# Three instead of two of eight column-block pairs of a gated feed-forward layer in seven block products

## The chip, the cores and the metric

One core of a Trainium2 chip. The metric is the device time of one execution in microseconds (us). The engines are PE (TensorE: matmuls, with PEld for its weight loads), DVE (VectorE), ACT (ScalarE), POOL (GpSimd) and SP (SyncE, whose queue issues the loads of the weights).

## The reference

Two layers over 256 tokens of width 2048, float32. Each layer is feed-forward 1, a mixer (stick-breaking attention in the first layer, causal pooling in the second), feed-forward 2, each behind a scaled residual and followed by a layer norm. There are thus four feed-forward layers, and these are what the change is about:

```python
def swiglu(x, w_in, w_out):
    a, gate = jnp.split(x @ w_in, 2, axis=-1)      # w_in: 2048 x 8192, split into 4096 + 4096
    return (jax.nn.silu(a) * gate) @ w_out         # w_out: 4096 x 2048
...
    x = layer_norm(DEEPNORM_ALPHA * x + FFN_RESIDUAL * swiglu(x, *ffn1[i]), *ln1[i])
    x = layer_norm(DEEPNORM_ALPHA * x + mixers[i](x), *ln2[i])
    x = layer_norm(DEEPNORM_ALPHA * x + FFN_RESIDUAL * swiglu(x, *ffn2[i]), *ln3[i])
```

## The kernel before, in words

Activations stay on the chip, transposed: features on the 128 partitions, the 256 tokens along the free dimension. To keep float32 accuracy each operand is split in two: ACT casts it to a rounded high part, DVE subtracts that from the operand to give the low part (`parts`, L323, for the weights here; L140 and L141 in `chunk`). High times high, high times low and low times high are accumulated in PSUM.

`ffn_in` (L447) computes the 8192 columns of `w_in` as eight groups of 512 features (one block of 512 columns of the first half and its partner in the gate's half):

- Group 0 comes first, by two calls of `gemm`, whose hooks also finish the layer norm before it.
- The middle groups go by **column units**. `feature(t)` (L520) is a block of 128 features: two units, one for the first half's 128 columns and one for the gate's. A unit is `column` (L327): one load of 1 MB, two casts and two subtractions of 128x1024, 32 matmuls (16 of 128x512, high weight with both parts of the activations, and 16 of 128x256, low weight with the high part) into one PSUM bank, an ACT copy of the bank (L350), one DVE add (L524), and a silu or, every second time, a multiply (L535). A group of 512 features is eight units.
- The last `SEVENS` groups go by **seven block products** (`Seven`): the 256 tokens are two halves of 128, the 2048 inputs two halves of 1024 and the two partner blocks of columns the third pair, so that a group is a 2x2 by 2x2 block product, done with seven products instead of eight and sums before and behind. `prepare` (L360) makes the sums of activations once per layer. `run` (L376) goes through eight steps, each with one load of 1 MB (L383), the split of the plain blocks, three combinations of weight blocks (L400), their splits, and seven products of three 128x512 matmuls each (L422 to L424), accumulated over the steps in seven PSUM banks. Behind the last step an ACT copy and seven DVE adds (L434) combine the banks. The result has tokens on the partitions; `gated` (L470) multiplies it with the gate and puts off eight PE transposes (L481) and two ACT copies, the "late" part.

Between the products of a run the code interleaves column units: `run` calls `between(i, h)` (L559) after the first four (h = 0) and the last three products (h = 1) of step i, except at the very end. The units before, between and behind the runs are taken in order from one list (`unit`, L543). Before the first run some units come early; the late part of a run comes in the first step of the next one. At the end `settle` (L458) splits the gated products for the output matmul, partly into the places of the activations' sums.

The buffers that count: three raw blocks of weights (`raws`), six pairs for split weights (`whis`, `wlos`), two for combinations (`sums`), four `wide` tiles, and eight PSUM banks, of which a run holds seven.

What sets the order: the code is not issued as it is written. A planner takes the instructions by priority (their order in the code), simulates times with its own costs, gives out buffers, and so writes each engine's order. Each engine then works through its list in that order.

Of the kernel before, what the change touches and what calls it, by code (L numbers as in the profile page):

```python
# [21 lines left out]
INNER = HEADS * P  # L22
WINDOWS = (2, 4, 8, 16)

SEVENS = 2
PARTS = ('', '_columns', '_seven')
ALPHA = 4 ** 0.25
SB_SCALE = P ** -0.5
# [10 lines left out]
def trunk(ctx: ExitStack, tc: tile.TileContext, a: dict, out: bass.AP):  # L39
# [407 lines left out]
    def ffn_in(w_in, w_columns, w_seven, norm, hooks=None):  # L447
# [69 lines left out]
        seven.prepare(1)  # L517
        todo = list(range(4, 4 * (ng - SEVENS)))

# [18 lines left out]
        units = []  # L538
# [4 lines left out]
        def unit():  # L543
            if not units:
                return
            go = units.pop(0)
            if held:
                go(held.pop())
            else:
                held.append(go())  # L550

        early = len(units) - 16 * SEVENS
        for _ in range(early // 2):
            unit()
        if hooks:
            hooks()
        lates = []

        def between(i, h):  # L559
            unit()  # L560
            if lates and (i, h) == (0, 1):
                lates.pop()()

        for grp in range(ng - SEVENS, ng):
            acts, gates = seven.run(w_seven, grp - ng + SEVENS, between)
            unit()
            lates.append(gated(grp, silu(acts, acts), gates))
# [9 lines left out]
    def ffn(p, i, ln, norm):  # L577
        gs = ffn_in(*(a[f'{p}ffn{i}_w_in' + x] for x in PARTS), norm)
        if norm is None:
            nc.sync.dma_start(vecs, a['vecs'])  # L580
        return sublayer_end(a[f'{p}ffn{i}_w_out'], gs, 0.5, f'{p}{ln}_g', f'{p}{ln}_b')
# [162 lines left out]
    def last(p, norm):  # L744
# [5 lines left out]
        def turn():  # L750
            for q in range(4):
# [6 lines left out]
                for m in range(2):  # L758
                    nc.scalar.copy(z[q][:, m, :], ps[m])

        gs = ffn_in(*(a[f'{p}ffn2_w_in' + x] for x in PARTS), norm, hooks=turn)
        for i, name in enumerate((f'{p}ln3_g', f'{p}ln3_b')):
            gb = res.tile([P, 4, 2 * W], F32, tag=f"xs{i}", name=f"gb{i}")
# [105 lines left out]
```

## Time and profile before

| | us |
|---|---|
| median of 3 runs | 2654.95 (2654.46 to 2655.19) |
| the profiled execution | 2653.92 |
| its span, first to last instruction | 2652.2 |
| PE busy in the span | 2632.2 |
| DVE busy | 1964.3 |
| ACT busy | 1476.5 |

The profile records one execution. Busy times of an engine are the union of its instructions' times; a matmul's recorded end is modelled and overlaps the start of the next. A row of a group of instructions reads: line, engine, operation, output and inputs, shape, count, busy time in us and mean ns of one, then the engine's idle time before them and what ended it. A row of a window reads: the stretch in us from the span's start, its length, then busy us (and instructions) of each engine, the granted clock, the share of the DMA engines and GB/s.

### The profile page before, as it was taken

The page shows a single profiled execution, that of the slowest core. Times are in us where ns is not written, and L with a number is a line of the kernel's source. Part 1 is how long each engine was busy: PE and PEld are TensorE (multiplying, and loading weights), DVE is VectorE, ACT ScalarE, POOL GpSimd, SP SyncE. Part 2 cuts the span into 40 slices and gives each one's busy share as a digit, 9 for nine tenths or more (in the row PEclk, how much of TensorE's full clock was granted, in tenths as well). Part 3 has the DMA queues.
Part 4 walks back from the last instruction along what each step waited for, and adds up shares of the span by engine and source line. Part 5 has one row for each costly group of instructions (what it writes and reads, how often), then busy time and mean ns, then how long its engine had stood idle before and what let it go on. Part 6 is the DMA issues. An engine that isn't in the chain of part 4 may idle for free.

```text
span 2652.2 us, 37769 instructions
## 1 busy us (share of the span) xinstructions
PE 2632.2 (99%) x15148; PEld 2303.4 (87%) x15148; DVE 1964.3 (74%) x2650; ACT 1476.5 (56%) x2094; POOL 11.9 (0%) x28
## 2 busy tenths in 40 slices
PE   9999999999999999999999999999999999999998
PEld 8888888899998888888988888889888998888886
DVE  8778766585689787665797886657878797888545
ACT  6556554466576565544655565445555575566432
POOL 0000000000000000000000000000000000000000
PEclk9999999999999999999999999999999999999999
DMA  7555555554455555555455555554555545555653
GB/s 269 193 178 206 182 201 187 189 178 165 151 177 191 189 195 192 201 183 197 169 189 198 192 190 191 191 191 165 201 188 177 191 159 191 192 192 207 221 195 121
DMA packets 71518, 499.54 MB, mean 188 GB/s; under 512 B 7984, under 2 KB 8624, under 8 KB 12080
## 3 DMA queue, kind: packets, MB, share of 16 engines
q1 hardware_dynamic: 70704, 495.05, 53.6%
q8 instruction: 118, 1.93, 0.3%
q0 software_dynamic: 640, 2.10, 0.2%
q14 instruction: 56, 0.46, 0.1%
HBM read 495.02 MB, written 2.10 MB: 187 GB/s over the span
## 4 chain that ended last, share of the span: by engine, by line
PE 98%; ACT 1%; DVE 0%; DMA 0%; SPq 0%; issue 0%; DVEq 0%; ACTq 0%
PE pc L341 23%; PE ps L164 21%; PE pc L345 12%; PE ps L167 10%; PE ps L159 4%; PE ps L158 4%; PE ps L160 4%; PE p L422 4%; PE p L423 4%; PE p L424 4%; PE y L805 2%; PE y L806 2%; PE y L804 2%; PE v L660 1%; PE v L658 1%; PE v L659 1%
## 5 line engine op out<-in xcount | busy, mean ns | idle before, releaser
L341 PE MATMUL pc<-xs,whi 128*128 128x512 f32 x2560 | 914.5, 397 | 3.7 <-ACT col L350 2.9
L141 DVE TENSOR_TENSOR wlo<-raw,whi 128x1024 fp32r<-128x1024 f32 (+1 forms) x498 | 596.7, 1202 | 423.8 <-ACT whi L140 423.0
L140 ACT CAST whi<-raw 128x1024 fp32r<-128x1024 f32 (+1 forms) x498 | 510.5, 1033 | 550.1 <-PE ps L164 343.8
L345 PE MATMUL pc<-xs,wlo 128*128 128x256 f32 x2560 | 694.0, 281 | 0.0
L341 PEld LDWEIGHTS pc<-xs,whi 128*128 128x128 f32 x2560 | 481.6, 189 | 116.8 <-ACT col L350 10.4
L325 DVE TENSOR_TENSOR wlo<-raw,whi 128x1024 fp32r<-128x1024 f32 (+1 forms) x448 | 503.0, 1144 | 47.4 <-ACT whi L324 28.9
L164 PE MATMUL ps<-g,whi 128*128 128x512 f32 x1536 | 534.9, 394 | 0.0
L324 ACT CAST whi<-raw 128x1024 fp32r<-128x1024 f32 (+1 forms) x448 | 432.8, 989 | 173.1 <-PE pc L341 153.4
L345 PEld LDWEIGHTS pc<-xs,wlo 128*128 128x128 f32 x2560 | 483.7, 189 | 13.0
L167 PE MATMUL ps<-g,wlo 128*128 128x256 f32 x1536 | 427.8, 280 | 0.0
L164 PEld LDWEIGHTS ps<-g,whi 128*128 128x128 f32 x1536 | 287.2, 187 | 65.3
L167 PEld LDWEIGHTS ps<-g,wlo 128*128 128x128 f32 x1536 | 289.7, 189 | 1.1
L350 ACT COPY col<-pc 128x512 f32<-128x512 f32 x160 | 93.9, 588 | 224.0 <-PE pc L341 222.0
L159 PE MATMUL ps<-xs,whi 128*128 128x258 f32 (+1 forms) x768 | 218.3, 284 | 0.0
L158 PE MATMUL ps<-xs,whi 128*128 128x258 f32 (+1 forms) x768 | 217.6, 283 | 0.0
L160 PE MATMUL ps<-xs,wlo 128*128 128x258 f32 (+1 forms) x768 | 216.5, 282 | 0.0
L164 PE MATMUL ps<-xs,whi 128*128 128x512 f32 x512 | 178.9, 396 | 0.9 <-ACT whi L140 0.9
L160 PEld LDWEIGHTS ps<-xs,wlo 128*128 128x128 f32 x768 | 146.2, 190 | 0.0
L159 PEld LDWEIGHTS ps<-xs,whi 128*128 128x128 f32 x768 | 145.4, 189 | 0.2
L158 PEld LDWEIGHTS ps<-xs,whi 128*128 128x128 f32 x768 | 144.6, 188 | 0.0
L167 PE MATMUL ps<-xs,wlo 128*128 128x256 f32 x512 | 141.0, 281 | 1.6 <-DVE wlo L141 1.6
L524 DVE TENSOR_TENSOR col<-col 128x256 f32<-128x256 f32 x160 | 67.7, 423 | 77.6 <-ACT col L350 76.6
(196 smaller groups left out, 3581.5 us busy)
## 6 DMA issues: line engine op xcount, KB each, us to landing
raw<-in_l_ffn_w_in_columns SPq DMA_DIRECT2D x160, 1024.0 KB, 4.9
raw<-in_l_ffn_w_out SPq DMA_DIRECT2D x127, 1024.0 KB, 4.9
raw<-in_l_ffn_w_in_seven SPq DMA_DIRECT2D x64, 1024.0 KB, 5.2
raw<-in_l_pool_w_in SPq DMA_DIRECT2D x32, 1024.0 KB, 4.9
raw<-in_l_ffn_w_in SPq DMA_DIRECT2D x28, 1024.0 KB, 4.9
raw<-in_l_sb_w_qkv SPq DMA_DIRECT2D x24, 1024.0 KB, 4.9
raw<-in_l_pool_w_out SPq DMA_DIRECT2D x16, 1024.0 KB, 4.9
raw<-in_l_sb_w_o SPq DMA_DIRECT2D x8, 1024.0 KB, 5.0
```

Source lines behind the costliest of these rows:

```text
L140: nc.scalar.copy(hi[:, i], src)
L141: nc.vector.tensor_tensor(out=lo[:, i], in0=src, in1=hi[:, i].bitcast(F32), op=ALU.subtract)
L158: nc.tensor.matmul(ps[:, :one], hi[:, cs], x[:, 0, :one], start=first, stop=False)
L159: nc.tensor.matmul(ps[:, :one], hi[:, cs], x[:, 1, :one], start=False, stop=False)
L160: nc.tensor.matmul(ps[:, :one], lo[:, cs], x[:, 0, :one], start=False, stop=last)
L164: nc.tensor.matmul(ps.rearrange("p (h n) -> p h n", h=2), hi[:, cs], x, start=first, stop=last)
L167: nc.tensor.matmul(ps[:, :T], lo[:, cs], x[:, 0], start=False, stop=False)
L324: nc.scalar.copy(hi, src)
L325: nc.vector.tensor_tensor(out=lo, in0=src, in1=hi.bitcast(F32), op=ALU.subtract)
L341: nc.tensor.matmul(ps.rearrange("p (h n) -> p h n", h=2), his[k], whole[k], start=k == 0, stop=k == KT - 1)
L345: nc.tensor.matmul(ps[:, :T], los[k], whole[k][:, 0], start=False, stop=False)
L422: nc.tensor.matmul(p, xh, hi, start=i == 0, stop=False)
```

## The change

The number of groups done in seven products goes from two to three (`SEVENS`, which also sets how the weights are laid out in memory before the launch). The units left per layer go from 40 to 32. Where the code took half of the units that the runs leave as early ones, it now takes four (the same number as before). Between the products of a run a unit now comes after the second part of each step (h = 1) and, in the last step, after the first part; before, one came after either part.

```diff
-SEVENS = 2
+SEVENS = 3
...
-        early = len(units) - 16 * SEVENS
-        for _ in range(early // 2):
+        for _ in range(4):
             unit()
...
         def between(i, h):
-            unit()
+            if h == 1 or i == 7:
+                unit()
             if lates and (i, h) == (0, 1):
                 lates.pop()()
```

In the code's order a layer was: four units, a run with 15 units between, one unit, a second such run, and five units behind it (one at once, one after the first `settle`, three at the end). Now it is: four units, three runs with eight units between and one unit after each, and one more after the first `settle`.

## Rows read from the trace of the kernel before

**Rows 1.** Page, head and part 1: busy us, share, instructions of each engine.

```profile
span 2652.2 us, 37769 instructions
...
PE 2632.2 (99%) x15148; PEld 2303.4 (87%) x15148; DVE 1964.3 (74%) x2650; ACT 1476.5 (56%) x2094; POOL 11.9 (0%) x28
```

**Rows 2.** Page, part 4: the chain that ended last, by engine.

```profile
PE 98%; ACT 1%; DVE 0%; DMA 0%; SPq 0%; issue 0%; DVEq 0%; ACTq 0%
```

**Rows 3.** Page, part 6: DMA issues, with count, KB each, us to landing.

```profile
raw<-in_l_ffn_w_in_columns SPq DMA_DIRECT2D x160, 1024.0 KB, 4.9
...
raw<-in_l_ffn_w_in_seven SPq DMA_DIRECT2D x64, 1024.0 KB, 5.2
```

**Rows 4.** Windows of the first and second feed-forward layer: both runs, the rest.

```profile
75.45:204.83 129.38, 129.38 (x682) 110.16 (x680) 100.93 (x118) 71.73 (x89) 0.00 (x0) 1.00 0.54 192
204.83:330.74 125.91, 125.49 (x658) 106.05 (x657) 102.36 (x131) 76.04 (x107) 0.00 (x0) 1.00 0.54 191
811.11:942.34 131.23, 129.95 (x682) 110.10 (x680) 107.99 (x130) 75.95 (x98) 0.00 (x0) 1.00 0.55 192
942.34:1068.26 125.92, 125.48 (x658) 106.06 (x657) 102.47 (x131) 75.83 (x107) 0.00 (x0) 1.00 0.54 191
330.74:359.82 29.08, 29.08 (x170) 25.49 (x169) 23.31 (x33) 19.35 (x32) 0.00 (x0) 1.00 0.64 220
```

**Rows 5.** Chain in order of time: start, us, the transposes behind the second run.

```profile
347.30 0.66 PE gt L481 x6
```

**Rows 6.** Groups of instructions by shape: DVE's work in units and runs.

```profile
L325 DVE TENSOR_TENSOR wlo<-raw,whi 128x1024 fp32r<-128x1024 f32 x384 | 461.9, 1220 | 45.6 <-ACT whi L324 28.7 <-PE pc L345 14.4 <-issue 0.5
...
L400 DVE TENSOR_TENSOR ta<-raw 128x1024 f32<-128x1024 f32 x64 | 78.2, 1222 | 18.8 <-DMA raw<-in_l_ffn_w_in_seven 18.1
...
L524 DVE TENSOR_TENSOR col<-col 128x256 f32<-128x256 f32 x160 | 67.7, 423 | 77.6 <-ACT col L350 76.6
...
L400 DVE TENSOR_TENSOR tb<-raw,ta 128x512 f32<-128x512 f32 x64 | 43.8, 685 | 0.1
...
L434 DVE TENSOR_TENSOR c<-p,su 128x512 f32<-128x512 f32 x16 | 11.0, 685 | 0.0
```

**Rows 7.** Timeline of DVE, end of first layer: start, us, instruction, count.

```profile
325.05 1.42 DVE L108 TENSOR_TENSOR g<-gw,g 128x256 fp32r<-128x256 f32 x4
...
329.68 1.28 DVE L434 TENSOR_TENSOR c<-p,u 128x512 f32<-128x512 f32 x2
...
338.56 3.49 DVE L325 TENSOR_TENSOR wlo<-raw,whi 128x1024 fp32r<-128x1024 f32 x3
```

**Rows 8.** Timelines of ACT and PE, second layer's first step; in brackets idle before.

```profile
813.23 1.05 ACT L324 CAST whi<-raw 128x1024 fp32r<-128x1024 f32 x1 [0.81 <-PE p L423]
...
814.71 0.58 ACT L350 COPY col<-pc 128x512 f32<-128x512 f32 x1
...
815.34 0.50 PE L341 MATMUL pc<-xs,whi 128*128 128x512 f32 x1 [1.26 <-ACT col L350]
```

**Rows 9.** Windows around the start of the second layer's runs.

```profile
773.16:829.18 56.02, 54.74 (x340) 48.75 (x339) 56.02 (x85) 41.95 (x70) 0.00 (x0) 1.00 0.55 188
788.61:811.11 22.50, 22.50 (x130) 19.66 (x129) 22.50 (x38) 11.73 (x17) 0.00 (x0) 1.00 0.50 167
811.11:827.05 15.94, 14.66 (x70) 11.78 (x69) 15.94 (x22) 13.26 (x19) 0.00 (x0) 1.00 0.50 174
```

**Rows 10.** Waits over the whole span: who, on whom, us, times, longest.

```profile
ACT whi L324 <- PE pc L341: 204.6, 129, 4.1
DVE wlo L325 <- ACT whi L324: 93.9, 102, 2.1
```

## The prediction

> **What bounds the kernel now.** I read the page first: TensorE is busy 99% of the span, VectorE 74%, ScalarE 56% [rows 1], and the chain that ended last lies 98% on TensorE [rows 2]. So the reader is to see a kernel that is a row of matmuls with hardly a hole; only fewer or shorter matmuls, or new holes, can change it. Next come the weights: each block of 1 MB lands about 5 us after its issue [rows 3]. The change reads the same megabytes in another form (a group is eight blocks either way: 160 and 64 of the two kinds now, 128 and 96 then), all issued by the same queue, so the total of DMA stays.
>
> Then I cut the first and second feed-forward layers into stretches [rows 4]: from the first seven-product matmul to that of the second run, from there to the run's last, and the rest up to the output product. They give the price of both forms of work. The third and fourth layer repeat the pattern.
>
> **What a group costs TensorE in each form.** The rest after the last run holds five units and eight transposes in 29.08 us [rows 4]. Transposes step by 0.66 / 6 = 0.11 us [rows 5], so eight take 0.88, and a unit takes (29.08 - 0.88) / 5 = 5.64 us. A group in plain columns is eight units (four features, two halves each): 45.1 us.
>
> The two runs of the first layer last 129.38 + 125.91 = 255.29 us with 16 + 15 units between them and one set of transposes: 255.29 - 31 x 5.64 - 0.88 = 79.6, or 39.8 per run. The second layer gives 131.23 + 125.92 - 174.84 - 0.88 = 81.4, or 40.7 [rows 4]. Mean 40.25 (a step of a run: 5.03), holes within the runs included. With its transposes a group as a run costs 40.25 + 0.88 = 41.1 us.
>
> So TensorE gets 45.1 - 41.1 = 4.0 us per layer, 16.0 us in the four layers; with the two layers' own run prices it is 4.4 or 3.5, 17.8 or 14.2 us in all. This is on the path that sets the end, and it is the term that the change is worth if no new hole opens.
>
> **What VectorE must do in the same time.** The change moves more than it removes. A column unit asks two subtractions of 1024, one add of 256 and half a multiply of 256. A step of seven products asks subtractions of 512, 1024, 1024, 512, 512, 1024 and 1024 for its splits and combinations. The rows say 1.22 us for 1024, 0.685 for 512, 0.42 for 256 [rows 6]. These overlap end to start: three of 1024 in a row take 3.49, so each further one adds (3.49 - 1.22) / 2 = 1.135; two of 512 take 1.28, so 0.60; four of 256 take 1.42, so 0.333 [rows 7].
>
> By steps: a unit 2 x 1.135 + 0.333 + 0.17 = 2.77; a step 4 x 1.135 + 3 x 0.60 = 6.34; the end of a run seven adds and two multiplies of 512 = 5.4. Check on the first run of before: 8 x 6.34 + 16 x 2.77 + 5.4 = 100.4 against 100.93 busy [rows 4]. It fits.
>
> After the change a run holds eight units (one in each step) and one behind it. VectorE: 50.7 + 9 x 2.77 + 5.4 = 81.0 us. TensorE: 40.25 + 0.88 + 9 x 5.64 = 91.9 us. VectorE's share rises from 78% (100.93 of 129.38) to 88%; it stays under TensorE's. ScalarE, even were all its 71.7 us of a long run left in the short one, would be at 78%. So neither becomes the bound by its sum. Cover for the seven products' splits is the unit of the step before: 5.64 us of TensorE against 6.34 us of VectorE, of which the first 1.7 us are enough to begin.
>
> **The rule against it.** The rows show a next operation that starts before the row of the last one has ended (3.49 us for three of 1.22) [rows 7]. The Trainium skill, "VectorE: DVE Perf Modes", section Terms, says that a pipeline flush follows each VectorE operation and the next can't issue until the pipe is empty. Read as whole durations one behind the other, a run would cost VectorE 8 x 6.94 + 9 x 3.07 + 9 x 0.685 = 89.3 us, 97% of TensorE's 91.9, and next to nothing of slack would be left. The trace doesn't agree with that reading, so the sum above goes by the steps.
>
> **Buffers and the bank.** Split weights have six buffer pairs. Before, a double-unit step fills 3.5 + 4 of them in 5.03 + 11.28 = 16.3 us; after, 3.5 + 2 in 5.03 + 5.64 = 10.7 us. A pair may stay 6 x 10.7 / 5.5 = 11.6 us against 13.0: a little less room to run ahead. Raw blocks: two in 10.7 us against three in 16.3, the same rate. Units share the one bank that seven products leave; now a whole step lies between two units, so its evacuation (0.58 us [rows 8]) is better hidden than before, and would add that much per unit if it were not. I take these three at nothing; if the run-ahead is too short, each of the 12 runs pays: bounds 0 (as now) to 1.26 us (the one hole a run opens with, below), I take 0.1, nearer to the steady steps of before, which have no such hole; 1.2 us.
>
> **The start of the runs.** In the second layer VectorE is busy without a break from 773.16 to 829.18 (56.02 of 56.02), because the sums of activations for the seven products, the end of the norm and four units come together; in the 22.50 us of those units it is full too [rows 9]. TensorE then waits 1.26 us for a bank that ScalarE empties late, behind a cast that itself waited for a buffer [rows 8]. But in 811.11 to 827.05 the planner ran 70 matmuls, some twelve products and one unit [rows 9], which is just what the new order asks there. So the new order should meet much the same lag. Bounds for each of the three layers that begin behind a norm: 0 to 4.5 us (VectorE's work at the start of layer two: sixteen operations of 512 for the sums 9.6, four units 11.1, first step 6.3, 27.0 together, against 22.50); I take 0.5, as the twelve-product stretch is the nearest row; 1.5 us.
>
> **The end of the runs.** Five units cover the end now; two will (11.3 us and 0.88 of transposes). VectorE must by then have done: last adds and multiplies 3.0, the rest of the two units' splits and sums 3.3, four of the first gate splits 1.3, the first block of the output weights 2.3: 9.9 us against 12.2. It fits with 2 us to spare, while before it was 23.31 of 29.08 [rows 4] with much that could wait. If the cover is gone, the path behind the last product (add, silu, multiply, transposes, copy: about 3 us) shows. Bounds 0 to 3 per layer, I take 0.75; 3.0 us. The three stalls cannot gain more than the holes already in the runs, which the two run prices span (3.6 us in all).
>
> **Sum.** -16.0 + 1.2 + 1.5 + 3.0 = -10.3 us. The profiled execution took 2653.92 us (span 2652.2 and 1.7 around it), so 2643.6; the median of the runs shown is 1.03 above that execution, so 2645 us.
>
> **Rivals.**
> - VectorE becomes the bound (the other side). It is in order, waits for ScalarE's casts (93.9 us over the kernel), and these wait for TensorE to free buffers (204.6 us) [rows 10]. In a run's stretch it has been at most 82% busy (107.99 of 131.23) [rows 4]. A run then takes 81.0 / share. At 87% it is 93.1, 1.2 us over TensorE's 91.9, and twelve runs eat 14; below 87% the change loses. At 85%: 95.3, 12 x 3.4 = 41, net +25: about 2680 us. At 82%: +67, 2722. Against it: the 56 us without a break [rows 9], and that those waits come of running ahead into full buffers, when nothing is late. Chance 0.17, most of it near 86%.
> - The ends eat the gain: 3 x 3.5 at the starts and 4 x 1.5 at the ends make 16.5, net 0: about 2655 us. For it: VectorE is full at the start, and cover falls from five units to two. Against it: the sums above. Chance 0.17.
> - Nothing is late and the holes in the runs go too: -17.8 and none of the stalls, 2637 us. Chance 0.15.
> - The planner orders the units away from the steps to which the code gives them, so that the mix of before and after is alike within a step: it cannot win back the three units per layer that no longer cover the end; by the sum the result is the forecast's, so it has no price of its own.
>
> **How the numbers follow.** The forecast has 0.51. What this kernel's measurement can tell from no change is 0.2%, 5.3 us: faster is under 2649.6, slower over 2660.3. Faster: nearly all of the forecast's and of the best case's, 0.65. Same: the ends' rival and the edges, 0.17. Slower: VectorE's rival and a little of the ends', 0.18. The range goes from 2635 (best case with 2 us more) to 2668 (the milder half of VectorE's rival), the forecast's own from 2638 to 2650.
>
> **What would show it.** Windows over the three runs of a layer: the second run about 92 us from first product to first product, VectorE near 81 busy in it; columns x128 and seven-product blocks x96 among the DMA issues; from the last product to the output product about 12.2 us with no hole over a microsecond; VectorE at some 2100 us over the span. If a run takes 95 us or more, with holes before product matmuls that end on VectorE's splits, VectorE's rival is right and the sum of steps is no guide to what an in-order engine can deliver; if the runs are 92 and the total doesn't fall, the ends are to blame.

## The result, and the profile after

After: 2632.8 us (2631.62 to 2633.31, 5 runs) against 2654.9 before; ratio 0.9917, 95% interval 0.9904 to 0.9931. The kernel is 22.1 us faster, where 10 had been forecast: right in sign, but below the lower end of the range (2635) and more than twice the forecast change.

The page of after: the span, the busy times that answer to [rows 1], the chain by engine that answers to [rows 2].

```profile
span 2630.5 us, 37467 instructions
...
PE 2612.0 (99%) x14828; PEld 2277.8 (87%) x14828; DVE 2084.0 (79%) x2798; ACT 1518.1 (58%) x2130; POOL 11.9 (0%) x28
...
PE 94%; DVE 3%; ACT 1%; issue 1%; DMA 0%; SPq 0%; DVEq 0%; ACTq 0%
```

VectorE has 120 us more to do, and TensorE is still busy 99%. VectorE's share of the chain rises from 0 to 3%: in places a product now starts when its split is just done. TensorE's busy time and its span have still shrunk by about the same, 20.2 and 21.7 us, so this has not opened holes. The DMA issues that answer to [rows 3] changed as the prediction counted them.

```profile
raw<-in_l_ffn_w_in_columns SPq DMA_DIRECT2D x128, 1024.0 KB, 4.9
raw<-in_l_ffn_w_in_seven SPq DMA_DIRECT2D x96, 1024.0 KB, 4.9
```

The windows that answer to [rows 4]: in the first layer the three runs and what follows up to the last transposes, then the first two runs of the second layer.

```profile
76.32:165.66 89.34, 89.34 (x458) 75.82 (x457) 78.66 (x92) 54.38 (x65) 0.00 (x0) 1.00 0.57 201
165.66:256.94 91.28, 90.99 (x466) 76.52 (x465) 82.38 (x98) 55.30 (x69) 0.00 (x0) 1.00 0.54 191
256.94:336.15 79.21, 79.21 (x402) 66.79 (x400) 74.03 (x94) 52.83 (x74) 0.00 (x0) 1.00 0.58 206
336.15:363.38 27.23, 27.23 (x161) 23.90 (x159) 23.97 (x39) 18.11 (x31) 0.00 (x0) 1.00 0.56 194
...
806.21:899.06 92.85, 90.78 (x457) 75.37 (x456) 86.76 (x106) 58.35 (x73) 0.00 (x0) 1.00 0.56 197
899.06:990.30 91.24, 90.95 (x465) 76.49 (x464) 82.80 (x98) 55.54 (x69) 0.00 (x0) 1.00 0.54 191
```

The middle run takes 91.28 us with VectorE 82.38 busy; 91.9 and 81.0 had been worked out. The last run is shorter because the planner kept three units, not two, for the stretch behind it, and it let output matmuls go ahead of the last transposes, so that this stretch shows no hole.

To see where the 22 us went, I took the time from each matmul's start to the next one's and summed it by kind over the four layers. The middle column is the first experiment below (two runs, but one unit per step).

| us, four layers | before | two runs, one unit per step | after |
|---|---|---|---|
| column units | 905.5 | 900.8 | 721.5 |
| seven products | 319.4 | 319.2 | 475.3 |
| transposes | 5.7 | 6.2 | 8.6 |
| median | 2654.9 | 2649.8 | 2632.8 |

The new interleave alone takes 4.7 us off the units and 4.4 off the three rows together. The third run then takes 179.3 us of units away and brings 156.0 of products and 2.4 of transposes: 20.9 us, 5.2 per layer, against 4.0 in the prediction. The first two runs are alike in the two kernels (in the first layer 78.10 and 85.66 us from first product to last, then 78.10 and 85.64), so it is the third run's own. TensorE's other matmuls take 3.6 us more than in before, 3.1 of it in the output product, into which the last transposes have moved.

### The profile page after: what moved, and what is told of

Same layout as the page of the kernel before. It is cut to its first block, busy times and chain, and to the rows that moved or that the text cites. A ratio compares the mean times of both kernels' runs of the same rounds, so it can differ in the third digit from the quotient of the medians.

```text
span 2630.5 us, 37467 instructions
## 1 busy us (share of the span) xinstructions
PE 2612.0 (99%) x14828; PEld 2277.8 (87%) x14828; DVE 2084.0 (79%) x2798; ACT 1518.1 (58%) x2130; POOL 11.9 (0%) x28
## 4 chain that ended last, share of the span: by engine, by line
PE 94%; DVE 3%; ACT 1%; issue 1%; DMA 0%; SPq 0%; DVEq 0%; ACTq 0%
PE ps L164 21%; PE pc L341 17%; PE ps L167 11%; PE pc L345 9%; PE p L422 5%; PE p L423 5%; PE p L424 5%; PE ps L159 4%; PE ps L158 4%; PE ps L160 4%; PE y L806 2%; PE y L804 2%; PE y L805 2%; DVE wlo L325 1%; PE v L660 1%
## 5 line engine op out<-in xcount | busy, mean ns | idle before, releaser
L141 DVE TENSOR_TENSOR wlo<-raw,whi 128x1024 fp32r<-128x1024 f32 (+1 forms) x498 | 595.9, 1200 | 407.7 <-ACT whi L140 407.2
L140 ACT CAST whi<-raw 128x1024 fp32r<-128x1024 f32 (+1 forms) x498 | 510.1, 1032 | 548.3 <-PE ps L164 336.6
L341 PE MATMUL pc<-xs,whi 128*128 128x512 f32 x2048 | 729.2, 396 | 1.4 <-ACT gw L483 0.7
L345 PE MATMUL pc<-xs,wlo 128*128 128x256 f32 x2048 | 554.9, 281 | 0.0
L325 DVE TENSOR_TENSOR wlo<-raw,whi 128x1024 fp32r<-128x1024 f32 (+1 forms) x448 | 487.9, 1103 | 39.3 <-ACT whi L324 21.6
L324 ACT CAST whi<-raw 128x1024 fp32r<-128x1024 f32 (+1 forms) x448 | 417.7, 959 | 164.0 <-PE pc L341 110.8
L341 PEld LDWEIGHTS pc<-xs,whi 128*128 128x128 f32 x2048 | 385.1, 189 | 87.3 <-ACT gw L483 2.6
L345 PEld LDWEIGHTS pc<-xs,wlo 128*128 128x128 f32 x2048 | 386.7, 189 | 11.4
L350 ACT COPY col<-pc 128x512 f32<-128x512 f32 x128 | 75.3, 588 | 151.6 <-PE pc L341 145.3
L422 PE MATMUL p<-whi,s 128*128 128x512 f32 x384 | 150.9, 395 | 0.9 <-ACT col L350 0.7
L423 PE MATMUL p<-whi,s 128*128 128x512 f32 x384 | 149.8, 392 | 0.0
```

The costliest lines, as they stand in the source:

```text
L140: nc.scalar.copy(hi[:, i], src)
L141: nc.vector.tensor_tensor(out=lo[:, i], in0=src, in1=hi[:, i].bitcast(F32), op=ALU.subtract)
L324: nc.scalar.copy(hi, src)
L325: nc.vector.tensor_tensor(out=lo, in0=src, in1=hi.bitcast(F32), op=ALU.subtract)
L341: nc.tensor.matmul(ps.rearrange("p (h n) -> p h n", h=2), his[k], whole[k], start=k == 0, stop=k == KT - 1)
L345: nc.tensor.matmul(ps[:, :T], los[k], whole[k][:, 0], start=False, stop=False)
```

## The experiments

**Only the interleave.** After with two runs; the units that are left over come behind the runs (by the trace 19 per layer, so the end has more cover than in either kernel).

```diff
-SEVENS = 3
+SEVENS = 2
...
         settle(range(8))
-        unit()
+        for _ in range(3):
+            unit()
```

> Two groups in seven products as before, but one column unit per step as after (the units left over come behind the runs). Theory (the gain is TensorE work alone: a group as a run costs about 39.7 us, as eight units 46): nothing, 2655 within 3 us. Rival (part of the gain, some 6 us of it, comes from fewer changes between products and units, not from the third run): about 2649 us.

Measured 2649.8 us, ratio 0.9982 (0.9973 to 0.9991). The rival has the amount: against 2654.6 for before in the same series, 4.7 us (2.4 to 7.2 by the interval) of the 22 have nothing to do with a third run. Its reason, fewer changes between the two kinds, does not hold, as the starts below show. The waits of TensorE's weight loads (who, on whom, us, times, longest) for ScalarE's copy of the units' bank in before, then the longest waits of products and that for the copy in this kernel:

```profile
PEld pc L341 <- ACT col L350: 10.4, 18, 1.7
```

```profile
PEld p L424 <- DVE wlo L325: 3.7, 6, 0.9
PEld p L422 <- ACT col L350: 3.5, 5, 1.3
...
PEld pc L341 <- ACT col L350: 1.0, 1, 1.0
```

Units have nearly stopped waiting for the copy, but at the layers' starts products now wait for it and for VectorE's splits; before has neither of these two rows.

Of two timelines of before, PE and ACT, one such place: three product matmuls, then a unit whose first matmul starts 0.37 us after the last product's, where 0.23 is the rule, while the copy of the unit before runs until 129.45.

```profile
129.12 0.39 PE L424 MATMUL p<-wlo,xs 128*128 128x512 f32 x1
129.49 0.50 PE L341 MATMUL pc<-xs,whi 128*128 128x512 f32 x1
...
128.86 0.59 ACT L350 COPY col<-pc 128x512 f32<-128x512 f32 x1 [2.20 <-PE pc L341]
```

By starts, the changes from products to units lose 7.0 us in before (132 changes, each against 0.231 us), 2.05 here (74) and 2.3 in after (118). After has nearly as many changes as before at a third of the loss, so it is not the change that costs; by the waits it is the bank that isn't empty when too little work lies between two units. In the table this gain of 5 us stands in the products' row, as the time up to a unit's first matmul counts to the product ahead of it, and the new waits at the starts cancel it there. Of the 4.7 us of the units' row, 2.6 are again waits for the bank (1.6 in first matmuls that take 0.1 us longer behind such a wait, 1.1 in two waits behind a unit); the rest is spread over thousands of matmuls by a few ns, without a wait that names a cause.

**The bank held longer.** Before and after, with each unit's copy done twice.

```diff
         nc.scalar.copy(c, ps)
+        nc.scalar.copy(c, ps)
         return c
```

> Before, with each column unit's bank emptied by the same ScalarE copy twice, so that the bank is held 0.48 us longer. Theory (what the change of the interleave gave, 4.7 us, was waiting for the one bank that a run leaves to units, where only three matmuls of products lie between two units, four or five times per layer): 4.5 x 4 x 0.48, about 9 us more, 2664 us. Rival (those 4.7 us are the price of changing between the two kinds of matmul, the bank has no part in it): 2655 us within 2.

> After, with the same copy done twice. Theory (a whole step of products lies between two units in after, so the bank is free in time): 2633 us within 3. Rival (ScalarE's time in the chain to VectorE counts in after, where VectorE is 90% busy): 2640 us or more.

Measured 2710.0 (ratio 1.021, 1.0196 to 1.0224) and 2646.1 (0.9968, 0.9955 to 0.998). For before neither reading has the number. Its waits (lines behind 350 stand one further down in these two kernels):

```profile
PEld p L423 <- ACT whi L324: 51.5, 49, 2.2
PEld pc L341 <- ACT col L351: 24.3, 27, 1.4
```

The wait for the bank grew from 10.4 to 24.3 us; by starts, the changes from products to units lose 17.1 us instead of 7.0, 10 more, where the theory had 9. But most of the loss is products that wait for casts: the second copy stands in ScalarE's list ahead of them. The edit did two things, so it doesn't isolate the bank. For after the rival has the number: 13 us are lost, although ScalarE is only some 60% busy there. TensorE's waits of that kernel, then the row of after that answers to the second:

```profile
PE p L423 <- ACT whi L324: 5.3, 7, 1.6
PE p L423 <- ACT col L351: 3.9, 4, 1.3
```

```profile
PE p L422 <- ACT col L350: 1.6, 3, 0.8
```

Products wait for casts above all, and for the bank too. That VectorE, 90% busy, has little time to catch up is argued, not shown; and the planner gave the units another order here (first and third runs hold eight instead of seven), so how the 13 us divide stays open.

**Cover taken from the third run.** After with a unit after either part of a step, as before.

```diff
-            if h == 1 or i == 7:
-                unit()
+            unit()
```

> Three groups in seven products as after, but two units per step in the code as before, so that the list of units is empty in the third run. Theory (a unit per step is what hides VectorE's 6.34 us per step behind TensorE): the third run goes at VectorE's pace, 50.7 us against some 39, and nothing covers the end, 15 to 22 us per layer: 2693 to 2721 us. Rival (the planner spreads the units as it needs them, wherever the code puts them): 2633 within 5 us.

Measured 2764.1 us (1.0412, 1.0398 to 1.0427). The theory has the sign and the place, but the price is 131 us over after where it had 60 to 88. Windows of the first layer: the part of the third run without units, and from its end to the last transposes.

```profile
310.09:373.45 63.36, 52.39 (x197) 37.71 (x195) 63.27 (x86) 39.59 (x60) 0.00 (x0) 0.92 0.39 133
373.45:390.77 17.32, 6.15 (x31) 5.47 (x32) 13.12 (x22) 7.17 (x14) 0.00 (x0) 0.69 0.52 182
```

VectorE is busy 63.27 of 63.36: the bound. Its list there holds splits for the output product too, which the estimate had left out, and behind the run TensorE is busy only 6.15 of 17.32. So the planner does not move units to where they are missing; their place in the code counts.

**More work for VectorE.** After, with the first combination of a step computed once more, or twice more (the result stays).

```diff
+                for _ in range(1):      # range(2) in the other kernel
+                    nc.vector.tensor_tensor(out=ta, in0=raw[:, 0:1].to_broadcast([P, 2, 512]), in1=raw[:, 1:4:2], op=ALU.subtract)
                 for dst, x, y in ((ta, raw[:, 0:1].to_broadcast([P, 2, 512]), raw[:, 1:4:2]),
```

> After, with the first weight combination of each step computed twice on VectorE (1.135 us more per step, 9.1 per run, the result is the same). Theory (VectorE can be filled to the brim): 82.4 + 9.1 = 91.5 us per run against TensorE's 91.3, 0 to 1.5 us per run lost, 2633 to 2651 us. Rival (an in-order VectorE that waits on casts can't be used above some 87%): 91.5 / 0.87 = 105 us per run, 2633 + 12 x 14 = about 2800 us.

> After, with the first weight combination of each step computed three times (18.2 us more of VectorE per run). Theory: VectorE is now the bound at 82.4 + 18.2 = 100.6 us per run, 9.3 over TensorE's 91.3: 2633 + 112 = about 2745 us (2735 to 2765). Rival (87% at most): 100.6 / 0.87 = 115.6 us per run, about 2925 us. If VectorE didn't matter at all: 2633 us.

Measured 2694.2 (1.0148, 1.0134 to 1.0162) and 2777.9 (1.0468, 1.0454 to 1.0482). The second runs of the first layer, with one and with two more:

```profile
160.57:256.18 95.61, 92.86 (x465) 75.86 (x464) 90.47 (x104) 54.42 (x70) 0.00 (x0) 1.00 0.54 187
```

```profile
166.55:269.07 102.52, 95.50 (x466) 75.39 (x464) 101.21 (x114) 54.12 (x68) 0.00 (x0) 1.00 0.50 175
```

VectorE reaches 95% and 99% of the run. The rival of 87% falls; but the theory that it can be filled for nothing falls as well. Where both engines have the same sum, a layer's second run pays by the starts some 3 us more for its products than in after, and its third 7 to 8. With two more, VectorE is the bound as the theory says, and the time is 13 us over the upper end of its 2735 to 2765.

**A fourth run.** After with four groups in seven products, a unit after steps 1, 3 and 5, two in the last step, as in after.

```diff
-SEVENS = 3
+SEVENS = 4
...
-            if h == 1 or i == 7:
+            if (h == 1 and i in (1, 3, 5)) or i == 7:
```

> Four groups in seven products, the 24 units that are left spread as four early ones and five per run. By TensorE's work: 24 x 5.63 + 4 x 39.7 = 294 us per layer against 299 in after, 2633 - 22 = 2611 us, if nothing were late. Theory (VectorE is the bound there: 24 x 2.77 + 4 x 56.1 + 9.6 = 300.5 us per layer, and the two kernels with more VectorE work have shown it 95 to 98% busy at best): 300.5 / 0.96 = 313 against 302 us per layer, about 2633 + 44 = 2677 us.

Measured 2701.8 us (1.0178, 1.0162 to 1.0193). VectorE is the bound, as the theory says, 267.84 of 274.46 us over the four runs of the first layer; the price is 69 us over after, 17 per layer instead of the 11 expected. Some 5.4 of the 17 are a hole before each layer's last transposes, which the theory did not hold.

```profile
77.04:351.50 274.46, 265.82 (x1275) 218.98 (x1274) 267.84 (x320) 172.78 (x220) 0.00 (x0) 0.99 0.53 188
```

**GpSimd for the combinations.** With four runs, and with three.

```diff
-                    nc.vector.tensor_tensor(out=dst, in0=x, in1=y, op=ALU.subtract)
+                    nc.gpsimd.tensor_tensor(out=dst, in0=x, in1=y, op=ALU.subtract)
                 ha, la = pair()
```

> As the kernel with four runs, but the three combinations of weight blocks per step are done by GpSimd, which is idle. VectorE falls by 32 x 2.34 = 75 us per layer to 226. Theory (VectorE was the bound and GpSimd is a free hand): TensorE is the bound again, 2611 to 2620 us. Rival (GpSimd takes several times VectorE's 2.34 us per step, or slows VectorE by its own traffic): GpSimd is the bound as soon as a step's combinations pass the step's 8.4 us, and the time is above 2677 us.

> After, with the three combinations of weight blocks per step done by GpSimd. VectorE falls from 82.4 to about 64 us per run. Theory (in after TensorE is the bound everywhere but in the holes at a layer's start): 2628 to 2633 us, only the 5 us of holes can go. Rival (VectorE's 90% already costs time spread over the runs): 2620 us or less. If GpSimd is slow or disturbs VectorE: above 2640 us.

Measured 2903.9 (1.094, 1.0925 to 1.0955) and 2725.4 (1.0267, 1.0253 to 1.0281): with four runs the rival, with three the last branch (GpSimd is slow or disturbs VectorE); theory and rival fall there. Groups of the kernel with three runs, then its timelines of POOL and DVE:

```profile
L400 POOL TENSOR_TENSOR ta<-raw 128x1024 f32<-128x1024 f32 x96 | 322.8, 3363 | 608.8 <-DMA raw<-in_l_ffn_w_in_seven 394.8 <-DVE wlo L325 136.5 <-ACT whi L324 37.3
...
L325 DVE TENSOR_TENSOR wlo<-raw,whi 128x1024 fp32r<-128x1024 f32 x352 | 565.1, 1625 | 15.3 <-ACT whi L324 13.1 <-PE pc L345 1.9
...
207.43 3.15 POOL L400 TENSOR_TENSOR ta<-raw 128x1024 f32<-128x1024 f32 x1 [6.02 <-DMA raw<-in_l_ffn_w_in_seven]
...
208.24 2.63 DVE L524 TENSOR_TENSOR col<-col 128x256 f32<-128x256 f32 x1
```

A combination of 1024 takes GpSimd 3.36 us on average where VectorE took 1.22, and VectorE's own subtraction rises from 1.22 to 1.62. An add of 256 that takes 0.42 in [rows 6] lasts 2.63 here and ends 0.3 us after the GpSimd operation beside it. A window in the runs of the first layer (the third busy time is VectorE's, the last GpSimd's):

```profile
165.00:250.00 85.00, 80.41 (x397) 66.02 (x397) 84.65 (x63) 48.65 (x60) 47.93 (x22) 0.98 0.48 170
```

VectorE is full with less to do, and GpSimd is busy little more than half of the time. So in this kernel the move costs time by slowing VectorE, not by GpSimd becoming the bound.

**Where the early units come from.** After with six early units (two fewer behind the runs); with six, taken from the last step of the first two runs; with five, from that of the first.

```diff
-        for _ in range(4):
+        for _ in range(6):      # range(5) in the third kernel
...
-            if h == 1 or i == 7:                   # unchanged in the first kernel
+            if h == 1 or (i == 7 and grp >= 7):    # grp >= 6 in the third kernel
```

> After, with six early units per layer instead of four, so that two fewer are left for the end. Theory (the holes at the start of a layer's first run are VectorE's backlog, 3.5 us in the second and 1.8 in the third layer, and more early units give it time; the end has VectorE 24.0 us busy of 27.2 and could lose two units of TensorE's cover only at a price): 4 us won at the starts, at the ends VectorE's 24.0 - 5.5 = 18.5 us against TensorE's 27.2 - 11.3 = 15.9, 2.5 us lost per layer: about 2639 us. Rival (the ends are covered by the output product anyway): 2629 us.

> Six early units as in the kernel before with that number, but the two are taken from the last step of the first two runs, so that the end has as many units as in after. Theory (the 30 us lost with six early units were the end's: 7.5 us per layer for want of cover, while the starts gained 3.3 and 1.8 us): the end is as in after, the starts gain, about 2628 us. Rival (VectorE at 82.4 - 2.8 = 79.6 us against TensorE's 85.7 in a run with one unit less is too close to its 95%): 2633 us or more.

> Five early units, the one more taken from the last step of the first run. Theory: the start holes of the second and third layer shrink by half or more, the rest as in after: 2630 us within 2. Rival (a run with a unit less is VectorE's): 2634 us or more.

Measured 2662.9 (1.0033, 1.0021 to 1.0046), 2646.7 (0.9969, 0.9958 to 0.998) and 2631.6 (0.9914, 0.99 to 0.9927). With six, the holes at the starts go (products of the second layer 117.6 instead of 120.9 us, of the third 117.6 instead of 119.4, by the starts), but the end of each layer opens. The first kernel's chain in the first layer, then PE's timeline:

```profile
352.33 0.75 DVE g L108 x2
353.08 0.58 DVE wlo L141
...
354.89 1.20 DVE c L434 x2
...
357.89 1.14 DVE wlo L141
359.02 0.67 DVE g L108 x2
359.69 0.61 DVE c L473
...
360.35 0.69 PE gt L481 x2
```

```profile
360.35 0.69 PE L481 MATMUL gt<-ident,c 128*128 128x128 f32 x2 [7.38 <-DVE c L473]
...
361.48 0.63 PE L164 MATMUL ps<-g,whi 128*128 128x512 f32 x1
...
362.12 0.63 PE L164 MATMUL ps<-g,whi 128*128 128x512 f32 x1
```

The transposes wait 7.38 us for the multiply behind the last product: VectorE's list has splits of output weights (L141) and of gated products (L108) between the combining adds (L434) and that multiply (L473). The theory had the place, at a third of its price (2.5 us per layer). With six and the old end, holes open at the joint of two runs, where the removed unit was (PE's timeline in the second layer, with the idle time before):

```profile
914.75 0.73 PE L424 MATMUL p<-wlo,s 128*128 128x512 f32 x2 [0.65 <-DVE wlo L325]
...
917.08 0.50 PE L422 MATMUL p<-whi,s 128*128 128x512 f32 x1 [0.77 <-ACT whi L324]
...
919.83 0.51 PE L424 MATMUL p<-wlo,s 128*128 128x512 f32 x1 [1.55 <-DVE wlo L325]
```

That is the rival: products sum to 122.6 us per layer there, 5 more than the 117.6 of the first kernel, which keeps the unit. Five is as good as after and not better: the intervals overlap nearly whole. Its time lies within the theory's 2630 within 2, but not by the theory's path: the products of the second layer cost 122.1 us (120.9 in after), those of the third 118.3 (119.4), so the holes at the starts did not shrink by half; one shrank and one grew. No kernel beat after beyond its interval.

## Why the prediction was wrong

- **What bounds the kernel**: right. TensorE's sum decides as long as nothing is late.
- **"I take these three at nothing" (buffers and the bank)**: the first step that failed. The prediction saw that the units' one bank would be easier to hand on, priced the copy at 0.58 us, and gave the edit no gain. The interleave alone gave 4.7 us by the medians; the units' waits for the bank fell from 10.4 to 1.0 us. The row of these waits was there to be read in before. That they are the whole of the 4.7 us is not shown: no edit changed the bank alone (the one that was tried also delayed the casts), and part of what the units won names no wait. The prediction's bound for what holes in the runs could give back, 3.6 us, was too small for the same reason: it was the difference between two layers that both hold waits for the bank, not the waits themselves. So its third rival (2637, chance 0.15), by which the holes go too, came nearest.
- **The price of a group**: right in kind, the second term that was mis-sized. Forecast 45.1 us of units against 41.1 of a run and its transposes; measured 44.8 against 39.6. The units hold. The run's 40.25 was an average over runs of before with their holes: the waits for the bank and the hole at a layer's start. By the starts a run averages 39.9 in before and, with other holes, in the kernel with two runs. The added one cost 39.0, near the 38.8 of 168 products at 0.231 us (an estimate from the starts), so it brings almost no hole with it. That makes 5.2 instead of 4.0 us per layer.
- **VectorE's sum by steps**: right. 81.0 us per run forecast, 82.4 and 82.8 measured, 90% of the run. As durations end to end it would have been 89.3. The rival's limit of 87% was too low: 95 to 99% were reached.
- **The stalls, 5.7 us together**: by places. In the runs 1.2 forecast; in the steady second run TensorE is busy 90.99 of 91.28. At the starts 1.5 was forecast for the three layers that begin behind a norm. By the starts, the products of the second and third layers cost 3.5 and 2.0 us more than the first layer's in after (120.9 and 119.4 against 117.4), and 1.6 and 1.1 more in before (80.7 and 80.2 against 79.1): 2.8 us are new; the fourth layer has next to nothing in either kernel. The kernel with two runs has nearly the same 3.5 and 1.9 (81.9 and 80.3 against 78.4), so this comes with the interleave, not with the third run, and the gain of the interleave above is net of it. PE's timeline of after at the second layer's start, with the idle time before:

```profile
813.28 0.50 PE L424 MATMUL p<-wlo,xs 128*128 128x512 f32 x1 [0.47 <-DVE wlo L325]
...
814.50 0.50 PE L422 MATMUL p<-whi,s 128*128 128x512 f32 x1 [0.48 <-ACT col L350]
...
817.18 0.50 PE L422 MATMUL p<-whi,xs 128*128 128x512 f32 x1 [0.82 <-ACT col L350]
```

- **The ends**: 3.0 us forecast, 3.6 paid, but in another way: no hole, the transposes stand between the output product's matmuls. The forecast that two units are cover enough is borne out: by the traces the planner left three in after, but two in the last two kernels with more early units, and no hole opens there either. The prediction's bound of 3 us per layer without cover, from a path of add, silu, multiply, transposes and copy, was wrong: in the first kernel with six early units one unit is left, and the hole is 7.4 us, since the path goes through VectorE's whole list. Where that list is fuller, two are not enough: the kernel with four runs has two there, and its hole of 5.4 us.

In sum: 4.4 us for the interleave that were taken at nothing, 20.9 instead of 16.0 for the third run, and 3.6 us given back instead of 5.7 give 21.7, which is what the span fell by.

## What to carry to other kernels

Take the price of added work from its steady stretch, not from an average that holds the waits the change does away with, and read the waits for a shared bank as a gain that a new order may bring. An engine in second place could be filled to some 90% of a steady run here with next to no loss, but not to where both sums meet; and work that covers the end of a stage is worth more than the path it seems to cover, because that path goes through everything queued on the engines between.

## What the runs showed of the hardware

GpSimd and VectorE got in each other's way: VectorE's 1024-wide subtraction of two tensors went from 1.22 to 1.62 us on average, and a 0.42 us add lasted 2.63 beside a GpSimd operation. In the kernel with three runs, 51 of the 128 adds of 256 (L524) began during a GpSimd combination and outlasted it; 50 of them ended 0.28 to 0.29 us after it did, whatever was left of it. The 64 adds that met none took 0.41. The Trainium skill, "SBUF — State Buffer", section "SBUF: two separate sides", says that the two share a pair of ports as an exclusive lock for the whole instruction, also for a VectorE operation with two SBUF inputs beside a GpSimd operation that reads SBUF; the trace agrees, these adds ending just after the GpSimd operation did.

In the first kernel with six early units, a hole cost more than its length: pairs of output matmuls start every 0.64 us behind the 7.38 us hole (361.48 to 362.12), and every 0.35 in after at the same place, where nothing is missing ahead of them. Two pairs of after (PE's timeline), and the window behind the hole:

```profile
354.04 0.39 PE L164 MATMUL ps<-g,whi 128*128 128x512 f32 x1
...
354.39 0.39 PE L164 MATMUL ps<-g,whi 128*128 128x512 f32 x1
```

```profile
360.35:366.00 5.65, 5.65 (x22) 4.94 (x23) 4.11 (x9) 1.75 (x4) 0.00 (x0) 0.60 0.43 171
```

The granted clock is 0.60 there, so most of this stretch ran at 1.2 of 2.4 GHz, after TensorE had been idle. In after it is 1.00 in every window shown. So in that kernel the end of a layer costs the hole, and then slower matmuls behind it, which neither the prediction's bound for the ends nor that kernel's own estimate held.
